# A two-layer decoder trunk on one NeuronCore: fewer side steps per unit of matmul, one attention block and half of a weight split moved to other stages

## Chip, cores and metric

The kernel runs on 1 core of one Trainium2 chip. The metric is the device time of one execution in microseconds (us); of several runs the median counts. One further execution was recorded by the hardware profiler, and all rows of the trace come from that one.

## What is computed

The reference is a residual stream of 2048 tokens of width 1024 that goes through two layers. Layer A is a gated MLP whose gate mixes the tokens of each chunk of 128 by a causal matrix. Layer B is attention in three groups of 8 heads with dilations 1, 4 and 16, each over a band of 128 keys back, with one shared set of keys and values; the three results are joined by a softmax over their log-sums. All of it is float32.

```python
# layer A
h = rms_norm(x, norm_g) * (1 + scale) + shift
u, v, z = split(h @ w_in, 3)                       # 1024 -> 3 x 2048
v = rms_norm(gelu(v), sgu_g)                       # then mixed over each chunk of 128 tokens
x = x + gate * ((gelu(u) * mixed(v) * silu(z)) @ w_out)
# layer B
k, v = split(h_kv @ w_kv, 2)                       # 6 heads each, rms_norm on k
q, z = split(h_b @ w_in)                           # 24 heads and 1024 for z, rms_norm on q
for g, d in enumerate((1, 4, 16)):                 # band attention on tokens taken d apart
    o[g], lse[g] = dilated_group_attn(q[g], k[g], v[g], d)
x = x + gate_b * ((sum(softmax(lse)[g] * o[g]) * silu(z)) @ b_w_out)
```

`shift`, `scale` and the gates come from a small product of `c`.

## The kernel before

**Quarters and products.** The 2048 tokens are taken in four quarters of 512; the code counts them from 0, this text from 1. For each quarter the kernel runs layer A, its output product (to x of layer B), then the shared keys and values, the queries of the three groups and z (`proj_B`, four blocks of 128 tokens each). Quarters 2 and 3 share their layer A (`layer_half`). Every float32 product is made of three matmuls: each operand is split (`split`, lines 272 and 273) by ScalarE into a rounded high part and by VectorE into the remaining low part, and high x high, low x high and high x low are added in PSUM (`mm3`, line 301). Most products are cut into 2 x 2 blocks and done with seven block products instead of eight, with weights `t1` to `t4` that are sums and differences of the blocks, written to memory beforehand.

**The stages that the change touches, in order of time:**
- `layer_half`: `dense_v` multiplies the v columns in two blocks (`b` = 4 and 5), seven products of 96 matmuls each. Then come eight gate groups `g`, each one `gate_block` for u and one for z, of seven products of 12 matmuls; their mixing matmuls (tile `pmh`, line 1468) read v once the norm over all v columns (`rvh`) is known.
- `layer_out(2)`: the output product of quarter 3 (`dense_o`, tiles `pd_o2a`, `pd_o2b`), seven products of 48 matmuls.
- `proj_B(2)`: keys and values (`kv_block`), and the queries of dilation 16 (`q_block(2)`), before `ahead` starts the loading of quarter 4's x into the only slot of the pool `one`.
- `layer_A(3)`: quarter 4's v products (`dense_s2`), then u and z (`dense_f`, lines 343 to 345, 16 blocks of 48 matmuls), then its output product.

**Side work.** What is not on the path of the current product is written as Python generators in the list `fillers`. Each `yield` ends a step. A product calls `tick(part)` after every few matmuls; it adds `rate[0] * part` to a counter and runs as many steps as the counter holds whole units, so that `rate[0]` is the number of steps per unit of tick. A unit is 24 matmuls in `dense_v`, `dense` and `dense_f` (0.25 per 6 matmuls), 12 matmuls in `gate_block` (0.25 per 3), and 21 in `dense_o`, `dense_s` and `dense_s2` (0.2857 per 6). `drain()` runs all steps that are left; `complete(g)` those of one generator. The steps set the order in which instructions are handed to a scheduler, which lays out each engine's queue and can let an instruction ahead whose data and buffer are there.

**The generators that matter here:**
- `combine_out` makes the weights `t1` to `t4` of layer A's output matrix: 8 items, each with two loads of 512 KB (tile `co`, line 451, issued one item ahead), four subtractions on VectorE (line 476), four splits (tile `cs`), and four stores of 512 KB (line 473). It has 2 steps before the first item and 3 per item. It is added behind the fifth product of block 4, once `sums_h` is complete, and is completed at gate group 2, where its pool gives way to the attention's (`ap`) and the generator `in_long` begins.
- `presplit` loads tiles of a weight matrix, splits them and stores both parts; `presplit_b` does that for layer B's output matrix (16 tiles `rawb` and `wbs`, to `wod`), which the last stage of the kernel reads.
- `attend` runs attention over blocks of 128 queries, two units (key heads) per block, in four stages per unit: `att_1` transposes keys and queries (tiles `kT`, `qT`), `att_2` makes scores and the exponentials (`ps`, `pr`), `att_3` transposes those (`pT`, finished by VectorE at line 1812 and GpSimd at 1813), `att_4` multiplies by the values (`po`, line 1838). Each stage is one step; the stages of different units interleave, so that three steps lie between `att_3` and `att_4` of a unit. Per call there are 4 x (units + 4) steps with the skew that is used here.
- `attend_local(Q, ..., both)` runs the four dilation-4 blocks of a quarter and, if `both`, the dilation-1 blocks behind them (`near`), for which `joint` first passes statistics through memory. With `both` false it runs only three of the four blocks.
- `earlier` runs beside quarter 4's u, z and output products: the fourth dilation-4 block of quarter 2 (`(1, 7)`), `joint(1)`, `near(1)`, then quarter 3's dilation 4 and 1. Every sixth step it also runs one of `presplit_b`. It holds 24 + 1 + 48 + 97 = 170 steps. The first three blocks of quarter 2's dilation-4 attention run in quarter 3's output product, 40 steps at rate 2.6.

Of the kernel before, what the change touches and what calls it, by code (L numbers as in the profile page):

```python
# [13 lines left out]
F32 = mybir.dt.float32  # L14
F32R = mybir.dt.float32r
# [20 lines left out]
def trunk(ctx, tc, out, x, c, a_ada_w, a_ada_b, a_norm_g, a_w_in, a_sgu_g, a_w_spatial,  # L36
# [387 lines left out]
                split(us[i - 1][:, 0, :], us[i - 1][:, 1, :], raws.pop(i - 1))  # L424
            yield

    def presplit_b():

        todo = [(b_w_out[k * P:(k + 1) * P, n * 512:(n + 1) * 512], wod[n, k]) for n in range(2) for k in range(KT)]
        return presplit(todo, own_tiles("b"))  # L430

    def own_tiles(nm):
        return lambda i, u: (wp.tile([P, 2, 512], F32R, tag="w", name=f"w{nm}s{i}") if u else
                             rp.tile([P, 512], F32, tag="raw", name=f"raw{nm}{i}"))
# [828 lines left out]
    def layer_A(Q, hA, m, sqv, j0):  # L1263
        if Q:
            ops, sums = sums_A(Q, hA, m)
            ev = [v_evac(Q, m, sqv, j) for j in range(4)]
            dense_s2(ops, (4, 5), f"v{Q}", lambda b, t, src, n: ev[2 * (b - 4) + n](t, src[:, 0:512]), sums)
            rate[0] = 4.9
        for j in range(j0, 0 if Q else 4):
            with ExitStack() as behind:  # L1270
                if Q == 0 and j == 1:
# [146 lines left out]
    def layer_half(ops, got):  # L1418

        nonlocal xp, ap_  # L1420
        ops.update({n: op_tile(n) for n in ("s2", "s1", "s4", "s3")})
        ops["22"] = op_tile("22", one)
        sqh.extend(sp.tile([P, 16], F32, tag="sqv", name=f"sqh{i}").rearrange("p (t j) -> p t j", t=4) for i in range(2))
        rvh = sp.tile([P, 16], F32, tag="sqv", name="rvh")[:, 0:8]
        sa = sums_h(ops, 12)
        next(sa)
        fillers.append(sa)
        co = combine_out()

        def others():  # L1430
            complete(sa)
            fillers.append(co)
            rate[0] = 1.3

        for b in (4, 5):
            rate[0] = 1.3
            dense_v(b, ops, lambda t, n, src, dst, junk, b=b: v_put(t, 2 * (b - 4) + n, src, dst, junk),
                    {} if b == 5 else {"22": others})
        store_late(0)
        for i in range(2):  # L1440
            nc.vector.tensor_reduce(rvh[:, 4 * i:4 * i + 4], sqh[i], AX.X, ALU.add)
        nc.gpsimd.tensor_scalar(rvh, rvh, 1.0 / AW, EPS, ALU.mult, ALU.add)
        nc.gpsimd.tensor_tensor(rvh, rvh, mhalf[:, 0:8], ALU.pow)
        rate[0] = 1.0
        for g in range(8):
            if g == 2:
                complete(co)
                cb.release()
                xp = None
                ap_ = ctx.enter_context(tc.tile_pool(name="ap", bufs=2, reuse_waits="tile"))  # L1450
                fillers.append(in_long())
                rate[0] = 1.5
            vch = []
            for half in range(2):
                v = wp.tile([P, 4, 256], F32, tag="w", name=f"vc{g}{half}")
                nc.sync.dma_start(v, vh[half * QT:(half + 1) * QT, g * 256:(g + 1) * 256]
                                  .rearrange("(c p) e -> p c e", p=P))
                for c in range(4):
                    i = 4 * half + c
                    nc.gpsimd.tensor_scalar(v[:, c, :], v[:, c, :], rvh[:, i:i + 1], None, ALU.mult)  # L1460
                vch.append(v)
            mt = {}

            def put_u(i, half, src):
                e = 2 * g + i
                pm = pst(f"pmh_{e}{half}")
                for c in range(4):
                    nc.tensor.matmul(pm[:, c * P:(c + 1) * P], vch[half][:, c, i * P:(i + 1) * P],
                                     wst[:, g, :], start=True, stop=True)
                m = mt[i, half] = sum_tile(f"mth_{e}{half}")[:, 0:512]  # L1470
                nc.vector.scalar_tensor_tensor(
                    m.rearrange("p (c t) -> p c t", t=P), pm.rearrange("p (c t) -> p c t", t=P),
                    late["sgu"][:, e:e + 1], late["b_s"][:, g, :].unsqueeze(1).broadcast_to([P, TPQ, P]),
                    ALU.mult, ALU.add)
                nc.scalar.activation(src, src, AF.Gelu_apprx_tanh)
                nc.vector.tensor_tensor(m, src, m, ALU.mult)

            def put_z(i, half, src):
                m = mt[i, half]
                nc.scalar.activation(src, src, AF.Silu)  # L1480
                if g == 7 and half == 0:
                    nc.vector.tensor_tensor(got["mt"][1][:, 6 + i, :], src, m, ALU.mult)
                    return
                nc.vector.tensor_tensor(m, src, m, ALU.mult)
                stores.append([0, lambda e=2 * g + i: nc.sync.dma_start(yd[half][:, e, :], m)])

            gate_block(g, 0, ops, put_u)
            gate_block(g, 1, ops, put_z, begin_y(got) if g == 7 else {})
        store_late(0)
# [65 lines left out]
    def proj_B(Q, hk, hb, keep, rest, ahead, ready):  # L1555
# [82 lines left out]
        if Q == 1:  # L1638
            rate[0] = 1.2
            slots = one.tile([P, 4, 2, 512], F32, tag="big", name="gbw")  # L1640
            fillers.append(delayed(ada_gate(b_ada_w[0], b_ada_b, 1, "gb", slots)))
        q_block(2)
        if Q == NQ - 1:
            fillers.append(wide_attention())
# [207 lines left out]

    def attend_local(Q, wrap=False, alt=False, both=True):

        bs = range(4 * Q, 4 * Q + (4 if both else 3))
        yield from attend([(1, b) for b in bs], wrap, int(alt), 1 + (wrap or alt), wrap or alt)
        if both:
            yield from joint(Q)
            yield from near(Q, wrap, alt)
# [198 lines left out]
    fillers.append(side_work())  # L2058
    rate[0] = 2.2
    def earlier():  # L2060
        p = presplit_b()
        for n, _ in enumerate(chain(attend([(1, 7)], True, 0, 2, True), joint(1), near(1, True), attend_local(2, True))):
            if n % 6 == 5:
                next(p, None)
            yield
        yield from p

    got, ops_h = {}, {}
    for Q in range(NQ):
        if Q in (0, 3):  # L2070
            if Q:
                one.release()
                xp = ctx.enter_context(tc.tile_pool(name="xp", bufs=4, side="right", reuse_waits="tile"))
                fillers.append(earlier())
                rate[0] = 0.0
            hk, hb, keep, rest, ahead_kv = layer_A(Q, hA, m, sqv, 1 if Q == 0 else 0)
        else:
            if Q == 1:
                layer_half(ops_h, got)
                drain()  # L2080
                rate[0] = 0.0
            else:
                fillers.append(attend_local(1, True, False, False))
                rate[0] = 2.6
            hk, hb, keep, rest, ahead_kv = layer_out(Q, got.pop("mt"), got.pop("yo", {}), got.pop("begun", None))
        if Q > 0:
            drain()
# [52 lines left out]
```

## Time and profile before

| | us |
|---|---|
| median of 3 runs (lowest to highest) | 2940.27 (2939.66 to 2943.56) |
| the profiled execution | 2939.51 |
| its span, first to last instruction | 2937.8 |
| TensorE busy in that span | 2863.8 (97%) |
| VectorE, ScalarE, GpSimd busy | 2216.8, 1639.8, 815.2 |

The mean granted clock of TensorE in that execution was 0.995. In the rows, PE is TensorE's matmuls, PEld its weight loads, DVE VectorE, ACT ScalarE, POOL GpSimd, SP the engine that issues all DMAs; `out<-in` are the program's tile names, and `L301` is line 301 of the kernel. A row of the groups ends with busy time, the mean ns of one instruction, and the engine's idle time just before the group, with who ended it. A row of the waits reads: engine, tile and line that waited, who released it, the sum of the waits in us, their count, the longest. Matmuls overlap in the pipeline: one of 512 columns is recorded with about 389 ns, while 24 of them in a row take about 5.4 us.

### The profile page before, as it was taken

The numbers are of one execution on the slowest core, as the hardware profiler recorded it, in microseconds if no ns is written. First come the engines' busy times: TensorE is split into PE (matmuls) and PEld (weight loads), VectorE is DVE, ScalarE is ACT, GpSimd is POOL, SyncE is SP. The second block draws the span as 40 slices with busy tenths as digits, with TensorE's granted clock in tenths as the row PEclk, the third lists the DMA queues.
The fourth block names the chain that finished last, engine by engine and source line by source line (L and its number), as shares of the span: only waits on it lengthen the run. The fifth ranks groups of instructions, "written<-read, shape, count | busy, mean of one in ns | idle before, by whom it ended". The sixth has DMA issues, their size and how long they took to land.

```text
span 2937.8 us, 45193 instructions
## 1 busy us (share of the span) xinstructions
PE 2863.8 (97%) x14450; PEld 2392.8 (81%) x14450; DVE 2216.8 (75%) x4104; ACT 1639.8 (56%) x3335; POOL 815.2 (28%) x1085
## 2 busy tenths in 40 slices
PE   8999999999999999999999999999999999999999
PEld 5888888877778887877888888878888888888887
DVE  6878567787677789867786868878879676888682
ACT  4334355766546666544553657756757367876441
POOL 1066513330021125003324035024435111122212
PEclk9999999999999999999999999999999999999999
DMA  9899856888945655687989768854636967789653
GB/s 322 293 332 343 293 188 206 277 294 298 325 164 163 208 175 170 234 326 224 311 302 320 237 201 268 286 181 155 213 105 230 353 203 231 251 271 331 222 169 111
DMA packets 388210, 718.74 MB, mean 245 GB/s; under 512 B 42011, under 2 KB 121085, under 8 KB 387589
## 3 DMA queue, kind: packets, MB, share of 16 engines
q1 hardware_dynamic: 387972, 715.87, 72.5%
q8 instruction: 114, 1.87, 0.3%
q14 instruction: 124, 1.01, 0.1%
HBM read 541.52 MB, written 174.20 MB: 244 GB/s over the span
## 4 chain that ended last, share of the span: by engine, by line
PE 73%; DVE 9%; DMA 7%; issue 4%; ACT 3%; POOL 2%; SPq 1%; POOLq 0%; DVEq 0%; ACTq 0%
PE pd_kv L301 7%; PE po L1838 3%; PE pd_o L301 3%; PE pd_v L301 2%; PE pd_z L345 2%; PE pd_z L344 2%; PE pd_z L343 2%; PE pd_o3a L301 1%; PE pd_u L345 1%; PE pd_u L343 1%; PE pd_u L344 1%; PE pd_v3a L301 1%; PE pd_vh4a L301 1%; PE pd_o1a L301 1%; PE pd_v3b L301 1%
## 5 line engine op out<-in xcount | busy, mean ns | idle before, releaser
L301 PE MATMUL pd_kv<-w_kv,hkh 128*128 128x512 f32 x672 | 209.5, 392 | 2.2 <-DVE w_kv L273 2.1
L1838 PEld LDWEIGHTS po<-kv,pT 128*128 128x128 f32 x1200 | 149.9, 193 | 30.6 <-POOL pT L1813 17.9
L1838 PE MATMUL po<-kv,pT 128*128 128x128 f32 x1200 | 156.2, 279 | 18.6 <-POOL pT L1813 14.2
L301 PEld LDWEIGHTS pd_kv<-w_kv,hkh 128*128 128x128 f32 x672 | 125.0, 188 | 29.6 <-DVE w_kv L273 3.2
L301 PE MATMUL pd_kv<-w_kv,hkl 128*128 128x512 f32 x336 | 131.0, 390 | 0.0
L1778 ACT ACTIVATE pr<-pr,stat,rt 128x256 f32<-128x256 f32 (+1 forms) x192 | 104.3, 545 | 40.0 <-DVE stat L1772 27.1
L1604 POOL TENSOR_SCALAR s_q<-s_q 128x4 f32<-128x4 f32 x96 | 25.8, 269 | 342.9 <-DVE s_q L1603 279.7
L272 ACT ACTIVATE w_q<-raw_q 128x512 fp32r<-128x512 f32 x144 | 88.5, 627 | 51.5 <-PE pd_kv L301 10.5
L273 DVE TENSOR_TENSOR w_q<-raw_q,w_q 128x512 fp32r<-128x512 f32 x144 | 97.4, 698 | 23.4 <-ACT w_q L272 22.8
L1460 POOL TENSOR_SCALAR vc<-vc,rvh 128x256 f32<-128x256 f32 x64 | 61.3, 975 | 190.1 <-DMA vc<-vh 138.2
L2029 PE MATMUL pf<-wo,yb 128*128 128x512 f32 x256 | 104.5, 408 | 0.2 <-ACT yb L1992 0.2
L343 PE MATMUL pd_u<-hAh,w_u 128*128 128x512 f32 x256 | 103.6, 405 | 0.0
L343 PE MATMUL pd_z<-hAh,w_z 128*128 128x512 f32 x256 | 103.6, 405 | 0.0
L2031 PE MATMUL pf<-wo,yb 128*128 128x512 f32 x256 | 100.8, 394 | 0.0
L345 PE MATMUL pd_z<-hAh,w_z 128*128 128x512 f32 x256 | 100.6, 393 | 0.0
L344 PE MATMUL pd_z<-hAl,w_z 128*128 128x512 f32 x256 | 100.5, 392 | 0.0
L344 PE MATMUL pd_u<-hAl,w_u 128*128 128x512 f32 x256 | 100.4, 392 | 0.0
L345 PE MATMUL pd_u<-hAh,w_u 128*128 128x512 f32 x256 | 100.4, 392 | 0.0
L2030 PE MATMUL pf<-wo,yb 128*128 128x512 f32 x256 | 100.1, 391 | 0.0
L1778 ACT ACTIVATE st_pr<-st_pr,stat,rt 128x256 f32<-128x256 f32 (+1 forms) x128 | 73.5, 576 | 38.0 <-DVE stat L1772 19.3
L1786 POOL TENSOR_TENSOR dg<-pr,ident 128x256 f32<-128x256 f32 x38 | 29.2, 768 | 212.2 <-ACT pr L1778 165.3
L1813 POOL TENSOR_TENSOR pT<-pT,dg 128x256 f32<-128x256 f32 x76 | 64.5, 852 | 78.3 <-DVE pT L1812 75.1
(1474 smaller groups left out, 9005.2 us busy)
## 6 DMA issues: line engine op xcount, KB each, us to landing
raw_q<-in_b_w_in_dram SPq DMA_DIRECT2D x144, 256.0 KB, 3.8
qt<-qd SPq DMA_DIRECT2D x96, 260.0 KB, 4.2
od<-ot SPq DMA_DIRECT2D x96, 256.0 KB, 3.1
w_o<-wtd SPq DMA_DIRECT2D x48, 512.0 KB, 5.4
raw_kv<-in_w_kv_dram SPq DMA_DIRECT2D x84, 256.0 KB, 3.6
kv<-kvd SPq DMA_DIRECT2D x75, 256.0 KB, 5.1
raw_u<-in_a_w_in_dram SPq DMA_DIRECT2D x64, 256.0 KB, 4.1
wt<-st_cw SPq DMA_DIRECT2D x64, 256.0 KB, 5.5
```

Of the source, the lines that this page charges most:

```text
L272: nc.scalar.activation(hi, src, AF.Copy)
L273: nc.vector.tensor_tensor(lo, src, hi.bitcast(F32), ALU.subtract)
L301: last_mm[0] = nc.tensor.matmul(pt, a, u[:, w, :], start=f, stop=e, skip_group_check=more)
L343: nc.tensor.matmul(pts[i], wh, hh[:, k, :], start=k == 0, stop=False)
L344: nc.tensor.matmul(pts[i], wh, hl[:, k, :], start=False, stop=False)
L345: nc.tensor.matmul(pts[i], wl, hh[:, k, :], start=False, stop=k == KT - 1)
L1778: nc.scalar.activation(pr[:, i, :], pr[:, i, :], AF.Exp, bias=mneg[:, i:i + 1], scale=u["rt"][:, h:h + 1], accum_out=lsum[:, i:i + 1])
L1813: nc.gpsimd.tensor_tensor(pT[:, :, 0, :], pT[:, :, 0, :], u["dg"][:, c * hp:(c + 1) * hp, :], ALU.add)
L1838: nc.tensor.matmul(po[:, h * P:(h + 1) * P], u["pT"][h // hp][:, h % hp, j, :], u["kv"][:, j, kh, 1, :], start=j == 0, stop=j == nk - 1)
L2029: nc.tensor.matmul(pt, yb[:, 0, k, :], w_[:, 0, :], start=k == 0, stop=False)
L2030: nc.tensor.matmul(pt, yb[:, 0, k, :], w_[:, 1, :], start=False, stop=False)
L2031: nc.tensor.matmul(pt, yb[:, 1, k, :], w_[:, 0, :], start=False, stop=k == KT - 1)
```

## The change

Five edits:
1. In `layer_half`, the rate is 1.3 for block 4, 0.8 from the point where `combine_out` is added to the end of block 5 (1.3 before), and 0.55 in gate groups 0 and 1 (1.0 before).
2. `attend_local` runs all four blocks also with `both` false, so block 7 of dilation 4 goes from quarter 4's u product (`earlier`) to quarter 3's output product, whose rate goes from 2.6 to 3.1.
3. `presplit_b` takes one column half `n`. Half 0 runs in quarter 3's `proj_B` beside `q_block(2)` and `kv_block(0)` at rate 0.8 (1.7 before, with nothing left to run), in a tile of the pool `one` (`spare_tiles`) instead of the weights' own buffers. Half 1 stays in `earlier`.
4. `earlier` holds 1 + 48 + 97 = 146 steps and runs one of `presplit_b` every tenth.
5. The rate in quarter 4's u and z products goes from 4.9 to 4.0.

```diff
-    def presplit_b():
-
-        todo = [(b_w_out[k * P:(k + 1) * P, n * 512:(n + 1) * 512], wod[n, k]) for n in range(2) for k in range(KT)]
-        return presplit(todo, own_tiles("b"))
+    def presplit_b(n, tiles):
+
+        return presplit([(b_w_out[k * P:(k + 1) * P, n * 512:(n + 1) * 512], wod[n, k]) for k in range(KT)], tiles)
+
+    def spare_tiles():
+        t = one.tile([P, 8, 512], F32R, tag="big", name="pre")
+        return lambda i, u: (t[:, 4 + 2 * (i % 2):6 + 2 * (i % 2), :] if u else t[:, i % 4, :].bitcast(F32))
...
             dense_s2(ops, (4, 5), f"v{Q}", lambda b, t, src, n: ev[2 * (b - 4) + n](t, src[:, 0:512]), sums)
-            rate[0] = 4.9
+            rate[0] = 4.0
...
         def others():
             complete(sa)
             fillers.append(co)
-            rate[0] = 1.3
-
+            rate[0] = 0.8
+
+        rate[0] = 1.3
         for b in (4, 5):
-            rate[0] = 1.3
             dense_v(b, ops, lambda t, n, src, dst, junk, b=b: v_put(t, 2 * (b - 4) + n, src, dst, junk),
...
-        rate[0] = 1.0
+        rate[0] = 0.55
         for g in range(8):
...
+        if Q == 2:
+            rate[0] = 0.8
+            fillers.append(presplit_b(0, spare_tiles()))
         q_block(2)
...
-        bs = range(4 * Q, 4 * Q + (4 if both else 3))
+        bs = range(4 * Q, 4 * Q + 4)
         yield from attend([(1, b) for b in bs], wrap, int(alt), 1 + (wrap or alt), wrap or alt)
...
     def earlier():
-        p = presplit_b()
-        for n, _ in enumerate(chain(attend([(1, 7)], True, 0, 2, True), joint(1), near(1, True), attend_local(2, True))):
-            if n % 6 == 5:
+        p = presplit_b(1, own_tiles("b"))
+        for n, _ in enumerate(chain(joint(1), near(1, True), attend_local(2, True))):
+            if n % 10 == 9:
                 next(p, None)
...
                 fillers.append(attend_local(1, True, False, False))
-                rate[0] = 2.6
+                rate[0] = 3.1
```

## The prediction

> **What bounds the kernel now.** I read the page's totals and chain first, then stage windows, then matmul groups and waits inside the stages that the change touches.
>
> ```profile
> span 2937.8 us, 45193 instructions
> PE 2863.8 (97%) x14450; PEld 2392.8 (81%) x14450; DVE 2216.8 (75%) x4104; ACT 1639.8 (56%) x3335; POOL 815.2 (28%) x1085
> PE 73%; DVE 9%; DMA 7%; issue 4%; ACT 3%; POOL 2%; SPq 1%; POOLq 0%; DVEq 0%; ACTq 0%
> ```
>
> TensorE is busy for 2863.8 of 2937.8 us. The change neither adds nor removes a matmul, so what it can win is inside the 74 us in which TensorE stands idle, plus what a lowered clock costs after such idle time. The profiled execution took 2939.51 us, 1.7 more than its span and 0.8 under the median 2940.27. The windows say where those 74 us lie (columns: window, length, then busy us of PE, PEld, DVE, ACT, POOL, granted clock, DMA share, GB/s):
>
> ```profile
> 680.00:720.00 40.00, 38.13 (x161) 30.77 (x160) 27.89 (x45) 23.09 (x49) 0.00 (x0) 0.96 0.80 280
> 720.00:780.00 60.00, 59.24 (x261) 48.73 (x260) 43.09 (x69) 35.34 (x71) 0.00 (x0) 1.00 0.92 328
> 780.00:820.00 40.00, 30.53 (x115) 24.31 (x114) 21.84 (x37) 20.46 (x42) 9.95 (x10) 0.83 0.80 287
> 804.00:871.00 67.00, 62.24 (x289) 51.99 (x288) 47.96 (x77) 28.87 (x49) 18.63 (x18) 0.95 0.51 179
> 820.00:890.00 70.00, 70.00 (x341) 59.02 (x340) 51.72 (x82) 27.77 (x44) 16.26 (x16) 1.00 0.45 153
> 960.00:1215.00 255.00, 247.66 (x1327) 209.72 (x1326) 217.30 (x432) 155.33 (x286) 66.73 (x80) 0.99 0.57 190
> 1520.00:1640.00 120.00, 116.72 (x621) 98.32 (x620) 84.75 (x161) 52.50 (x115) 36.93 (x56) 0.99 0.88 313
> 1677.00:1740.00 63.00, 63.00 (x279) 52.17 (x279) 40.97 (x66) 34.79 (x62) 21.75 (x44) 1.00 0.61 190
> 1930.00:2245.00 315.00, 299.40 (x1775) 259.58 (x1774) 261.28 (x601) 200.98 (x403) 135.13 (x190) 0.99 0.52 166
> 1940.00:1950.00 10.00, 7.65 (x38) 6.56 (x38) 8.91 (x17) 2.87 (x4) 0.21 (x1) 0.83 0.46 143
> 2245.00:2340.00 95.00, 93.89 (x477) 79.14 (x478) 70.75 (x144) 42.26 (x84) 25.19 (x30) 1.00 0.91 337
> ```
>
> Output combinations run from 680 to 820: 12.1 us of idle TensorE (1.9 + 0.8 + 9.5), and a clock of 0.96 and 0.83. Quarter 4's u and z products with attention beside them, 1930 to 2245, hold 15.6 us. Quarter 3's output product (1520 to 1640) holds 3.3, and the dilation-16 query product with the first keys (1677 to 1740) none. (The code counts quarters from 0; I say quarter 1 to 4.)
>
> **Part 1, combinations at fewer steps.** Matmul groups between 680 and 820 (busy us, mean ns | idle before), then two waits of the same stretch:
>
> ```profile
> L301 PE MATMUL pd_vh5a<-w_vh5t,op 128*128 128x512 f32 x24 | 8.2, 505 | 4.7 <-ACT w_vh5t L272 4.7
> L301 PE MATMUL pd_vh4a<-w_vh4t,ops 128*128 128x512 f32 x24 | 7.6, 479 | 1.9 <-ACT pd_vh4a L1405 1.9
> L301 PE MATMUL pd_vh5a<-w_vh,ops 128*128 128x512 f32 x24 | 5.9, 396 | 0.8 <-DVE w_vh L273 0.8
> L301 PE MATMUL pd_vh4a<-w_vh4t,op 128*128 128x512 f32 x24 | 5.6, 389 | 0.0
> L1468 PE MATMUL pmh<-wst,vc 128*128 128x128 f32 x4 | 1.4, 459 | 4.8 <-POOL vc L1460 4.8
> ```
> ```profile
> DVE co L476 <- DMA co<-in_a_w_out_dram: 11.5, 8, 3.5
> ACT w_vh5t L272 <- DVE co L476: 5.8, 1, 5.8
> ```
>
> An undisturbed run of 24 matmuls takes 5.6 us. The first two rows take 8.2 and 7.6, so 2.6 and 2.0 us of lowered clock ride on their 4.7 and 1.9 us of idle time. The cause is in the waits: VectorE waits 11.5 us for combination loads, and what is queued behind it (weight splits, evacuations) comes late. Removable here: 4.7 + 2.6, and 1.9 + 2.0 + 0.8, 12.0 in all. The 4.8 before pmh stays: it waits for the norm of the last v column, which the change does not touch.
>
> How far the new rates thin the stream:
>
> ```profile
> 720.15 5.44 PE pd_vh5a L301 x24
> ```
>
> Here 24 matmuls, which are one unit of tick in the v products, last 5.44 us; a gate block's unit is 12 matmuls, 2.72. A combination item is 3 steps: 3 / 1.3 x 5.44 = 12.6 us before, 3 / 0.8 x 5.44 = 20.4 after, in the gate blocks 3 / 0.55 x 2.72 = 14.8. Loads are issued one item ahead, so they get 7.8 us more to land. I take the 7.3 us around pd_vh5a as gone, and half of the other 4.7, since the first items run ahead of their place in the program and would meet the same traffic: -9.6.
>
> Against that, work moves. Of 26 steps, 4 x 1.3 + 14 x 1.3 = 23.4 were over by the end of the v products; now 4 x 0.8 + 14 x 0.8 = 14.4 are. The rest takes 11.6 / 0.55 = 21 of the 28 units of the first two gate groups: (26 - 14.4) / 3 = 3.9 items, in about 67 us from 804 to 871. Per item there are four subtractions and four splits' subtractions:
>
> ```profile
> L273 DVE TENSOR_TENSOR cs<-co,cs x32: 678/682/694, 706.4 to 819.2; 128x512 fp32r<-128x512 f32 x32
> L476 DVE TENSOR_TENSOR co<-co x16: 680/691/693, 683.4 to 791.1; 128x512 f32<-128x512 f32 x16
> ```
>
> Thus 4 x 0.69 + 4 x 0.68 = 5.5 us of VectorE, 21.4 for 3.9 items. The window 804 to 871 has 47.96 already, 2.7 of it from combinations, so about 66.7 of 67 would be filled. Part can slide into 720 to 780 (43.09 of 60) or past 871. The lower bound of the loss is 0, as in 820 to 890 (51.72 of 70, no idle); the upper comes from 960 to 1215, where VectorE is 85% busy and TensorE loses 7.3 us: at 85%, 66.7 needs 78.5 us, a loss of 11.5. I take 5. Part 1: -4.6.
>
> **Part 2, the dilation-4 pair leaves quarter 4.** Block 7 is two units. It now stands alone at the head of quarter 4's attention:
>
> ```profile
> 1943.48 0.80 PE L1764 MATMUL ps<-kT,qT 128*128 128x256 f32 x2 [2.35 <-DVE kT L1721]
> 1962.77 1.16 PE L1838 MATMUL po<-kv,pT 128*128 128x128 f32 x8 [1.46 <-POOL pT L1813]
> 1965.41 1.16 PE L1838 MATMUL po<-kv,pT 128*128 128x128 f32 x8 [1.48 <-POOL pT L1813]
> 1608.83 2.08 PE L1838 MATMUL po<-kv,pT 128*128 128x128 f32 x8 [1.74 <-POOL pT L1813]
> ```
> ```profile
> L1838 PE MATMUL po<-kv,pT 128*128 128x128 f32 x344 | 44.9, 281 | 12.0 <-POOL pT L1813 11.9
> L1838 PE MATMUL po<-kv,pT 128*128 128x128 f32 x96 | 13.6, 290 | 2.0 <-POOL pT L1813 2.0
> ```
>
> Its three waits, 5.3 us, leave quarter 4 with it. So does the low clock after the first, 0.83 over 1940 to 1950: 1.7 us, of which I count 1.5. The other waits of po there are 11.9 - 2.9 = 9.0 us over 344 / 16 = 21.5 less 2 units, 0.46 each, with three steps of 5.44 / 4.9 between pT and po, 3.33 us. In quarter 3's output product (a unit of tick is 21 matmuls, 4.76 us) three steps are 3 x 4.76 / 2.6 = 5.49 us, and 96 / 16 = 6 units lose 2.0, 0.33 each. At rate 4.0 the three steps are 4.08 us. By geometry each of eight waits would shrink by 0.75, 6.0 in all; by the line through the two rows it is 0.05 over 19.5 units, 0.9. I take 1.5, near the rows: spacing plainly isn't all of it. Quarter 4: -8.3 (ends -6.8 and -12.8).
>
> In quarter 3's product the three steps shrink to 3 x 4.76 / 3.1 = 4.61 us for 8 units: by the same line 0.39 x 8 = 3.1, 1.1 more than 2.0, and the enlarged tail (as at 1608.83) makes it +2. Ends: 0, and 8 x 1.12 (9.0 over eight waits) - 2.0 + 1.7 of clock, +8.7.
>
> **A rule against the rows.** The row at 1943.48 has 2.35 us of idle, and the clock falls all the same. The Trainium skill, "TensorE: Matmul & The Clock Gate", sections "What's actually happening" and "HAM oscillation — how this bites in real kernels", says that the clock halves after an idle window of about 3.4 us and asks only that no gap exceed that. By that rule neither the pair nor the 1.9 us before pd_vh4a would cost clock, and the sum would be 2.5 us smaller: 2932. The trace disagrees, so the sum keeps the rows.
>
> **Part 3, half of the last weights in layer B.** Eight of sixteen splits move from quarter 4 to 1677 to 1740:
>
> ```profile
> L273 DVE TENSOR_TENSOR wbs<-rawb,wbs 128x512 fp32r<-128x512 f32 x16 | 11.6, 726 | 2.7 <-ACT wbs L272 2.7
> L1042 SPq DMA_DIRECT2D xa<-in_x_dram x4: 327/428/430, 1641.8 to 1643.1; - x4
> L1049 ACT ACTIVATE sqj<-xa x8: 616/622/624, 1738.3 to 1767.0; 128x512 f32<-128x512 f32 x8
> L858 PE MATMUL pt_a<-ident,xa x32: 270/272/273, 1802.4 to 1842.9; 128*128 128x128 f32 x32
> ```
>
> Eight times 0.73 brings VectorE there to 46.8 of 63, 74%, the share at which 820 to 890 lost nothing: 0. ScalarE has 34.79 of 63 and room for as many. The new tile takes the one slot that quarter 4's x now enters at 1642, so those four loads go behind the last store, near 1740, and on SP the next query weights queue behind them. ScalarE's squares start some 10 us later; TensorE needs their result at 1802, 35 us after the last square, so the cover holds. Were it gone, the delay of 10 us would be paid. The u and z products have 32 units of tick, so quarter 4's own output product is left with 146 - 32 x 4.0 = 18 steps instead of 170 - 32 x 4.9 = 13; it idles for 1.1 us in 95 now. I give both together +0.5; ends 0 and +4.
>
> **Sum.** -4.6 - 8.3 + 2 + 0.5 = -10.4 on 2939.51, 2929.1; with 0.8 for the median, **2930**. Less than 0.2%, 5.9 us, can't be told from no change.
>
> **Rivals.** (a) Nothing is paid back: the gate blocks and quarter 3 absorb the moved work free and all 12.0 go. -12.0 - 12.8, 2916. For it: 820 to 890 has no idle time at all. Against: 66.7 of 67 us on VectorE.
> (b) The rates do not do what they say: a rate fixes only the place in the program's order, and loads and subtractions are let ahead as slots come free (the first subtraction runs at 683.4, and block 5 only begins at 720.15). The combination waits stay, 5 is paid in the gate blocks only where work really moved (say 2), and the result is -8.3 + 2 + 0.5 + 2, 2936.5, within what can't be told from no change.
> (c) Slower: VectorE becomes the bound of the first two gate groups. Price 11.5, and the clock at 0.83 as in 780 to 820 over those 78 us, 13 more, in place of 5: -10.4 + 19.5 = +9.1, 2949. It decides once the gate groups lose over 5 + 10.4 + 5.9 = 21 us. For it, the full 67 us; against it, 85% cost only 7.3 us in 255, with 0.99 of the clock.
>
> **Chances.** Forecast 0.52 (its own range 2922 to 2938), (a) 0.17, (b) 0.17, (c) 0.11, others 0.03. Faster by over 0.2%, below 2934.4: some 0.42 of the first, (a), and 0.05 of (b), 0.64; within: 0.22; slower: (c) and the tails of the others, 0.14. Range 2917 to 2944: it takes in nearly all of (a), and of (c) the half where the price stays under 20.
>
> **What would show it.** Right: no wait of ACT for co, idle before pd_vh5a under 1 us, clock near 1 from 780 to 800; combinations until about 870 with some idle TensorE in the gate groups; no kT wait near 1943; po idle in 1930 to 2245 near 8 us; no idle at 1677 to 1740. Wrong: combination waits at the same places, over 10 us idle between 815 and 890, or po waits in quarter 3's product of over 5 us.

## The result, and the profile after

The changed kernel takes 2908.44 us (median of 4 runs, 2903.27 to 2911.30), the kernel before 2941.91 beside it on the same chip (4 runs, 2939.66 to 2946.48): a ratio of 0.9882 with a 95% interval of 0.9862 to 0.9902. The forecast was 2930.0 and its range began at 2917: the direction was right, but the gain is over three times the one forecast, and even rival (a), where nothing is paid back, stopped at 2916. The profiled execution took 2910.12 us, with a mean granted clock of 0.998 (0.995 before).

The page's totals and chain of the kernel after:

```profile
span 2908.3 us, 45236 instructions
PE 2851.9 (98%) x14450; PEld 2386.6 (82%) x14450; DVE 2205.5 (76%) x4104; ACT 1639.2 (56%) x3335; POOL 819.7 (28%) x1085
PE 79%; DVE 6%; DMA 5%; ACT 4%; issue 4%; POOL 1%; SPq 0%; POOLq 0%; ACTq 0%; DVEq 0%
```

The span is 29.5 us shorter. TensorE's idle time (span less PE) fell from 74.0 to 56.4, by 17.6; its busy time fell by 11.9 with the same 14450 matmuls. Most of the latter is clock, by an estimate from the two mean clocks: 0.3% of 2908 is 8.7 us. VectorE's share of the chain fell from 9% to 6%.

The windows that answer to the prediction's, kernel after (columns as there):

```profile
680.00:720.00 40.00, 37.22 (x156) 30.05 (x155) 23.80 (x38) 19.97 (x43) 0.00 (x0) 0.96 0.68 227
720.00:780.00 60.00, 60.00 (x266) 49.70 (x265) 39.02 (x61) 35.21 (x71) 0.00 (x0) 1.00 0.83 295
780.00:820.00 40.00, 37.59 (x171) 30.75 (x170) 30.32 (x49) 22.52 (x48) 12.39 (x10) 1.00 0.92 311
798.00:865.00 67.00, 64.59 (x309) 53.87 (x308) 64.00 (x103) 36.93 (x64) 22.36 (x18) 1.00 0.78 276
1507.00:1628.00 121.00, 116.86 (x654) 100.31 (x653) 88.36 (x175) 56.56 (x128) 47.90 (x68) 0.97 0.89 309
1675.00:1735.00 60.00, 60.00 (x266) 49.71 (x265) 42.94 (x71) 34.69 (x64) 19.51 (x40) 1.00 0.90 306
1931.00:2209.00 278.00, 277.35 (x1647) 241.27 (x1646) 229.72 (x540) 177.50 (x358) 117.59 (x166) 1.00 0.48 155
```

The 9.5 us of idle time and the 0.83 of the clock at 780 to 820 are gone, and so is nearly all idle time of quarter 4's u and z products: 0.65 us in 278, against 15.6 in 315. Idle time is left at 680 to 720 (2.8 us, 1.9 before), before pmh (within 798 to 865) and in quarter 3's output product, which has a lower clock than before (0.97, it was 0.99).

A fixed window holds other work after the change, so the sum is made by stages, each from its first product to the first product of the next. Kernel before: block 5 of the v products, gate groups 1 and 2, gate groups 7 and 8, quarter 3's output product, quarter 4's u, z and output products.

```profile
719.99:804.71 84.72, 79.25 (x338) 64.63 (x336) 58.17 (x93) 48.10 (x98) 0.00 (x0) 0.96 0.93 328
804.71:895.33 90.62, 85.86 (x402) 71.83 (x400) 63.61 (x102) 37.89 (x63) 26.22 (x26) 0.96 0.46 159
1102.54:1214.27 111.73, 106.31 (x566) 89.47 (x564) 100.42 (x202) 63.92 (x116) 36.97 (x45) 0.98 0.55 187
1519.83:1677.29 157.46, 153.67 (x790) 128.95 (x789) 114.39 (x212) 76.18 (x161) 38.72 (x60) 0.99 0.85 295
1931.42:2384.89 453.47, 435.81 (x2446) 373.57 (x2445) 366.13 (x801) 269.18 (x537) 164.33 (x228) 0.99 0.61 204
```

The same five of the kernel after:

```profile
722.29:798.45 76.16, 76.16 (x338) 63.08 (x336) 46.75 (x74) 44.33 (x90) 0.00 (x0) 1.00 0.86 297
798.45:885.50 87.05, 84.64 (x401) 70.60 (x400) 77.13 (x125) 44.20 (x75) 29.69 (x26) 1.00 0.69 242
1093.95:1202.33 108.38, 105.40 (x565) 89.40 (x564) 98.44 (x203) 67.08 (x118) 42.23 (x48) 0.98 0.58 200
1507.41:1675.45 168.04, 163.41 (x865) 138.63 (x864) 126.40 (x241) 83.06 (x180) 51.91 (x76) 0.98 0.82 279
1931.07:2355.20 424.13, 420.83 (x2370) 361.49 (x2368) 342.61 (x763) 250.83 (x505) 154.75 (x212) 1.00 0.59 199
```

| stage | before | after | change | forecast |
|---|---|---|---|---|
| v products, blocks 4 and 5 | 165.16 | 157.27 | -7.9 | -9.6 |
| gate groups 1 and 2 | 90.62 | 87.05 | -3.6 | +5 |
| gate groups 7 and 8 | 111.73 | 108.38 | -3.4 | 0 |
| quarter 3's output product, and quarter 4's u, z and output | 610.93 | 592.17 | -18.8 | -6.3 |
| all else | | | +4.2 | +0.5 |

The last two stages are added up, because the pair that moved takes its own matmuls along: 75 of them now run in one and no longer in the other. "All else" is small differences over many stages. Single recordings differ by as much where the code is the same: block 4 of the v products takes 78.15 to 82.27 us in the ten that run it as the kernel after does, and all that follows quarter 4's output product takes 542.87 and 553.29 us in two of one kernel.

### The profile page after: what moved, and what is told of

It reads as the page before. It is cut to its first block, busy times and chain, and to the rows that moved or that the text cites. A ratio compares the mean times of both kernels' runs of the same rounds, so it can differ in the third digit from the quotient of the medians.

```text
span 2908.3 us, 45236 instructions
## 1 busy us (share of the span) xinstructions
PE 2851.9 (98%) x14450; PEld 2386.6 (82%) x14450; DVE 2205.5 (76%) x4104; ACT 1639.2 (56%) x3335; POOL 819.7 (28%) x1085
## 4 chain that ended last, share of the span: by engine, by line
PE 79%; DVE 6%; DMA 5%; ACT 4%; issue 4%; POOL 1%; SPq 0%; POOLq 0%; ACTq 0%; DVEq 0%
PE pd_kv L301 8%; PE po L1844 4%; PE pd_o L301 3%; PE pd_v L301 2%; PE pd_z L345 2%; PE pd_z L344 2%; PE pd_z L343 2%; PE pd_u L343 2%; PE pd_u L345 2%; PE pd_u L344 2%; PE pd_o3a L301 1%; PE pd_v3b L301 1%; DMA qt<-qd 1%; PE pf L2035 1%; PE pf L2037 1%
```

## The experiments

Theories at the start: **the prediction's** (combination loads that land late; a line through two stages for the spacing), against **a queue** (in block 5 the weight loads stand behind the combination's DMAs on SP) and **a distance** (a wait before po appears only where the chain of work from `att_3` to pT outlasts the time that three steps give it, so one rate decides over nearly all of the waits). In the expectations theory S is this distance, theory L the load of the eight splits that left quarter 4, and theory P the pair that stood alone.

### One part undone, from the kernel after

The rate of quarter 4's u and z products back at 4.9:

```diff
-            rate[0] = 4.0
+            rate[0] = 4.9
```

> The changed kernel with one number set back: 4.9 steps per unit of tick in quarter 4's u and z products instead of 4.0. Theory S (spacing): attention's last product waits when the chain behind the transposes (5.3 us on average before, 4.7 after) is longer than its distance in the queue (5.2 before, 6.0 after), so the closer steps alone bring most of the waits back: 6 to 12 us of idle TensorE in u and z, 2917 to 2922. Theory L (load): the eight weight splits that left made the chain short, so with them gone the rate hardly matters: under 3 us of idle, 2908 to 2912. Theory P (the lone pair): under 3 us as well.

Ratio to the kernel before 0.9916 (0.9892 to 0.9940). Its quarter 4 stages:

```profile
1926.20:2362.18 435.98, 425.37 (x2370) 363.85 (x2368) 344.41 (x763) 248.01 (x502) 148.63 (x212) 0.99 0.58 194
```

435.98 against 424.13: the same instructions take 11.9 us longer, 7.3 of it idle TensorE (10.61 against 3.30). Four waits before po hold 6.2 us of the idle time, one of them 4.1. This is what theory S expected, and the one number is worth more than the whole gain forecast, 10.4, of which it was given 1.5. The stages are read from one recorded execution each; in whole runs the difference is 0.0034, 10 us, with intervals that overlap.

All sixteen splits back in quarter 4, one every sixth step (`presplit_all` does what `presplit_b` did in the kernel before):

```diff
-            fillers.append(presplit_b(0, spare_tiles()))
...
-        p = presplit_b(1, own_tiles("b"))
+        p = presplit_all()
...
-            if n % 10 == 9:
+            if n % 6 == 5:
```

> The changed kernel with all sixteen splits of the last weights back in quarter 4 (one every sixth step, in the weights' own buffers) and none in layer B. Theory L: the po waits come back, 6 to 12 us of idle TensorE in u and z, 2917 to 2922. Theory S: at most 3 us, 2908 to 2913. Either way the stretch of the dilation-16 queries stays without idle time.

Ratio 0.9889 (0.9874 to 0.9903), where the kernel after has 0.9862 to 0.9902. Quarter 4's stages take 426.81 (+2.7), the two stages together 592.21 (592.17 after). That is theory S again. With the pair gone and the rate at 4.0, the place of the splits is worth 2 to 3 us in quarter 4 (the six recordings that run quarter 4 as the kernel after does take 423.71 to 424.81) and nothing that shows in whole runs.

The pair back in quarter 4, at the head of `earlier` (the output product's rate goes up so that the steps still end with the product):

```diff
-        bs = range(4 * Q, 4 * Q + 4)
+        bs = range(4 * Q, 4 * Q + (4 if both else 3))
...
-        for n, _ in enumerate(chain(joint(1), near(1, True), attend_local(2, True))):
+        for n, _ in enumerate(chain(attend([(1, 7)], True, 0, 2, True), joint(1), near(1, True), attend_local(2, True))):
...
-                rate[0] = 3.1
+                rate[0] = 2.6
...
-            rate[0] = 2.0
+            rate[0] = 2.7
```

> The changed kernel with block 7's two units back at the head of quarter 4's attention; quarter 3's output product gets its old rate 2.6, and quarter 4's output product 2.7 instead of 2.0, so that the 170 steps end within it. Theory P: the three waits and the low clock return, 5.3 + 1.5 us, and the others with them if the pair displaced what followed; quarter 3's product wins 2 to 3; in all 2912 to 2916. Theories S and L: about 2 to 4 us of the pair's own waits and none of the others, less what quarter 3's product wins: 2907 to 2911.

Ratio 0.9862 (0.9847 to 0.9877): undoing this part costs nothing, and perhaps it gains, which no theory expected. The last set comes back to it.

The combinations back at 1.3 and 1.0:

```diff
-            rate[0] = 0.8
+            rate[0] = 1.3
...
-        rate[0] = 0.55
+        rate[0] = 1.0
```

> The changed kernel with the combinations back at 1.3 steps per unit through block 5 and 1.0 in the gate groups. If the thinner stream alone freed block 5, its 8.5 us come back there and some 3 before the first mixing matmul: 2919 to 2922, with the stages behind gate group 2 unchanged. If part of it is the queue's order having changed for other reasons, less than 5 us: 2908 to 2913.

Ratio 0.9930 (0.9915 to 0.9945): 0.0048 above the kernel after, 14 us. Block 5, then gate groups 1 and 2, then 7 and 8 take 82.52, 93.77 and 113.62 us, against 76.16, 87.05 and 108.38: 18.3 in all. The third of these stages begins some 280 us behind the last combination, and no theory named it. Part of the second is spread: the six recordings with the thick stream's code there take 90.4 to 93.8 us.

### One part done, from the kernel before

The rate alone (4.0, and 2.7 in the output product behind it, so that the steps end there):

```diff
-            rate[0] = 4.9
+            rate[0] = 4.0
...
-            rate[0] = 2.0
+            rate[0] = 2.7
```

> The kernel before with one thing changed: 4.0 steps per unit in quarter 4's u and z products (and 2.7 instead of 2.0 in its output product, so that all 170 steps end there). Theory S: the po waits of the later units go, 6 to 9 us won, 2931 to 2936. Theory L: under 2 us won, 2938 to 2942, since all sixteen splits are still there.

Ratio 0.9954 (0.9941 to 0.9966), 13.5 us. Quarter 4's stages:

```profile
1932.36:2374.41 442.05, 433.38 (x2445) 371.43 (x2444) 364.96 (x801) 260.31 (x532) 163.49 (x228) 1.00 0.64 210
```

-11.4, of it 9.0 of idle time (17.66 to 8.67). The po waits of its u and z products, then those of the kernel before and of the kernel after, show what went:

```profile
L1838 PE MATMUL po<-kv,pT 128*128 128x128 f32 x288 | 35.6, 275 | 0.4 <-POOL pT L1813 0.4
```
```profile
L1838 PE MATMUL po<-kv,pT 128*128 128x128 f32 x352 | 46.1, 281 | 12.2 <-POOL pT L1813 12.2
```
```profile
L1844 PE MATMUL po<-kv,pT 128*128 128x128 f32 x288 | 35.0, 275 | 0.0
```

12.2 us of waits become 0.4 by the rate alone, with the pair still in place. (At 4.0 some units that ran here run in the output product instead, so there are 18 of them and not 22. That product's idle time goes from 2.0 to 6.0 us, only 0.8 of it before po.) The gain is more than theory S expected, 6 to 9 us.

The pair alone (block 7 out of `earlier` and into quarter 3's output product, at rate 3.1), and the splits alone (half of them in layer B, the rest every tenth step), each with the change's own lines for it:

```diff
-        bs = range(4 * Q, 4 * Q + (4 if both else 3))
+        bs = range(4 * Q, 4 * Q + 4)
...
-        for n, _ in enumerate(chain(attend([(1, 7)], True, 0, 2, True), joint(1), near(1, True), attend_local(2, True))):
+        for n, _ in enumerate(chain(joint(1), near(1, True), attend_local(2, True))):
...
-                rate[0] = 2.6
+                rate[0] = 3.1
```

> The kernel before with block 7's pair alone moved to quarter 3's output product at rate 3.1. Theory P: 5.3 + 1.5 us and more leave quarter 4, 2 to 3 come to quarter 3: 2930 to 2937. Theories S and L: the pair's place is taken by the next units, which wait as much: 2938 to 2942.

```diff
+            fillers.append(presplit_b(0, spare_tiles()))
...
-            if n % 6 == 5:
+            if n % 10 == 9:
```

> The kernel before with eight of the sixteen weight splits moved to layer B beside the dilation-16 queries. Theory L: quarter 4's waits fall by 6 or more, 2930 to 2935. Theory S: by less than 2, 2938 to 2942. Nothing is lost at the dilation-16 queries in either.

The pair: 0.9980 (0.9967 to 0.9993), 5.9 us; quarter 4's stages get 12.5 us shorter, quarter 3's product 6.3 longer. This is what theory P expected; S and L had nothing won. The splits: 1.0001 (0.9989 to 1.0013), and 453.39 against 453.47 in quarter 4, against theory L.

The combinations alone:

```diff
-            rate[0] = 1.3
+            rate[0] = 0.8
...
-        rate[0] = 1.0
+        rate[0] = 0.55
```

> The kernel before with the thinner combination stream alone. The prediction's own sum for this part was 4.6 us won (9.6 won in the v products, 5 lost in the gate groups). If the gate groups take the work for nothing, as the trace of the changed kernel suggests, 11 to 13 us: 2928 to 2931. If what was seen there hangs on the other edits, 2935 to 2938.

Ratio 0.9931 (0.9905 to 0.9957), 20.3 us. The three stages:

```profile
723.08:799.24 76.16, 76.16 (x337) 63.06 (x336) 46.82 (x75) 44.48 (x90) 0.00 (x0) 1.00 0.87 297
799.24:886.13 86.89, 84.56 (x402) 70.59 (x400) 77.12 (x125) 44.30 (x75) 29.62 (x26) 1.00 0.69 242
1093.91:1199.99 106.08, 103.62 (x566) 88.10 (x564) 98.28 (x203) 66.85 (x118) 41.93 (x48) 1.00 0.60 202
```

-8.6, -3.7 and -5.6, 17.9 in all, in line with the 18.3 that undoing it cost. It is more than the 11 to 13 us expected. The rest lies in stages of unchanged code: quarter 3's output product takes 153.31 us instead of 157.46, block 4 takes 82.27 instead of 80.44.

### What is behind these numbers: one execution each, from the kernel after

Each of these four kernels was executed once (2919.18, 2918.44, 2914.65 and 2905.01 us in this order, with 2940.80 for the kernel before), so only their stages are read.

Why gate groups 7 and 8? All steps after the combinations run by one counter, and what is left in it decides which small group of matmuls each later step follows. The thick stream leaves 0.798 in it, the thin one 0.198. This kernel keeps the thick stream and changes only that remainder, where `in_long` begins:

```diff
-            rate[0] = 0.8
+            rate[0] = 1.3
...
-        rate[0] = 0.55
+        rate[0] = 1.0
...
                 rate[0] = 1.5
+                rate[1] = 0.19812
```

> The changed kernel with the thick combination stream (1.3 and 1.0), and the step counter's fraction set to 0.198 where attention joins the gate groups, as the thin stream leaves it (the thick one leaves 0.798). In the runs so far gate groups 6 and 7 took 111.7 to 113.6 us with the thick stream and 106 to 108.4 with the thin one, though no combination is left there. If the fraction alone shifts attention's steps against the gate products and so makes the difference: 106 to 108.5 for the two groups, block 5 still at 82 to 85. If it comes from the combinations' later end (buffers, stores): 111 to 114.

Gate groups 7 and 8:

```profile
1103.06:1210.72 107.66, 104.95 (x565) 89.45 (x564) 98.39 (x203) 67.25 (x118) 40.91 (x47) 0.98 0.59 201
```

107.66, where the thick stream had 113.62; the kernels with the thin stream's remainder have 106.0 to 108.4, all others 111.7 to 113.6. Block 5 stays at 83.15. So some 3 to 6 us of the gain have nothing to do with combinations and came by luck: they are the place at which later steps happen to fall. Which of those steps matters was not taken apart.

Does VectorE bind the gate groups (rival (c))? Here more combinations are pushed into them, 0.4 steps in block 5 and 0.73 in the groups; and, in the second kernel, fewer, 0.8 and then 1.0 steps, so that the stream ends early but comes thick:

```diff
-            rate[0] = 0.8
+            rate[0] = 0.4
...
-        rate[0] = 0.55
+        rate[0] = 0.73
```

> The changed kernel with 0.4 steps per unit through block 5 and 0.73 in the gate groups, so that 18.8 of 26 steps, some 6.3 items and 34 us of VectorE, fall into the first two groups, beside about 56 us that it has there anyway, in 81 us of matmuls. If a full VectorE binds there as the slow rival said: the two groups take 90 to 100 us instead of 87.1, with waits for weight splits. If weights are split far enough ahead for that not to matter, or the queue lets the work go ahead of its place: 86 to 89.

```diff
-        rate[0] = 0.55
+        rate[0] = 1.0
```

> The changed kernel with 1.0 steps per unit in the gate groups (as before) but 0.8 in block 5. If the 0.8 alone frees block 5: 76.2 us there, and 1.0 in the gate groups costs at most 2. If the lower rate behind it matters too, because its items are let ahead into block 5: 78 to 84 us.

Gate groups 1 and 2, of the first and of the second:

```profile
799.88:889.77 89.89, 85.95 (x401) 71.50 (x400) 83.81 (x137) 48.00 (x82) 30.87 (x23) 0.98 0.84 299
```
```profile
795.29:887.68 92.39, 87.09 (x401) 71.27 (x400) 77.92 (x125) 43.57 (x75) 30.71 (x26) 0.98 0.65 227
```

The first takes 2.8 us more than the 87.05 of the kernel after, just between my two expectations, with VectorE 93% busy over 90 us. But the only wait of TensorE there is the one before pmh, in the first 24 us (3.9 us, 2.3 in the kernel after). Where VectorE is fullest, TensorE has no idle time:

```profile
824.00:854.00 30.00, 30.00 (x142) 25.10 (x142) 29.50 (x48) 16.67 (x28) 10.34 (x8) 1.00 0.89 321
854.00:889.77 35.77, 35.77 (x175) 30.19 (x174) 34.61 (x57) 19.39 (x32) 5.05 (x5) 1.00 0.84 295
```

The thick stream, with the same VectorE work as the kernel after (77.92 and 77.13), takes 5.3 us more: TensorE waits 2.2 us before pmh and 3.1 for ScalarE's splits of gate weights. So it is not the amount of VectorE work that costs. That those splits come late because the combinations come more closely fits, but was not taken apart. My expectation for the second, at most 2, missed. Block 5 takes 76.16 in both.

The distance theory says that waits shrink along a curve: strongly at first, then not at all once the distance covers the chain. A rate halfway tells that from a straight line:

```diff
-            rate[0] = 4.0
+            rate[0] = 4.45
```

> The changed kernel with 4.45 steps per unit in quarter 4's u and z, halfway between before and after. Quarter 4 from u through its output product took 424.1 us at 4.0 and 436.0 at 4.9. By a wait that is the excess of the chain over the distance, with the chain's length spread from 2.6 to 7.8 us, the loss rises faster than the rate: 426 to 429, po waits of 1 to 3 us. By a straight line: 430 to 431.

```profile
1924.83:2353.61 428.78, 422.02 (x2369) 362.03 (x2368) 345.72 (x763) 250.81 (x505) 153.22 (x212) 1.00 0.59 197
```

424.13, 428.78 and 435.98 at 4.0, 4.45 and 4.9: the first half of the way costs 4.7 us, the second 7.2. A straight line would put the halfway kernel at 430.1. It lies 1.3 us under that, hardly more than the 1.1 us by which the six recordings at 4.0 differ: it leans to a curve and does not prove one.

### Is there a better version? The pair again, on one chip

The kernel after, and the kernel with the pair back (edit as above), timed side by side:

> The changed kernel once more, beside the next one on the same chip: 2903 to 2912.

> The changed kernel with the pair back in quarter 4 (rates 2.6 and 2.7 in the two output products). If moving the pair was worth what the prediction gave it at the new rate (its own three waits and the low clock, 6.8, less 2 in quarter 3): some 5 us slower than the changed kernel. If it only exchanges one place for another: within 3 us of it. If the fuller output product of quarter 3 costs more than the pair's waits did at 4.0 steps: 4 to 8 us faster.

0.9867 (0.9851 to 0.9884) and 0.9878 (0.9856 to 0.9900), medians of 2903.42 and 2907.84: no difference clear of the intervals. Quarter 3's output product and quarter 4's stages, first of the kernel after:

```profile
1503.75:1670.40 166.65, 161.81 (x865) 137.13 (x864) 126.94 (x241) 83.02 (x179) 51.97 (x76) 0.99 0.82 280
1926.57:2350.79 424.22, 420.99 (x2369) 361.64 (x2368) 342.07 (x763) 251.32 (x505) 156.04 (x212) 1.00 0.59 200
```
```profile
1506.65:1660.42 153.77, 151.37 (x789) 127.63 (x788) 115.64 (x211) 75.02 (x159) 39.73 (x60) 1.00 0.85 293
1915.59:2352.55 436.96, 431.45 (x2446) 370.66 (x2444) 358.10 (x793) 256.74 (x525) 163.13 (x228) 1.00 0.60 197
```

The sums are 590.87 and 590.73. At the rate of 4.0, moving the pair carries 12.9 us of work and waits from one stage into the other and wins nothing. The better ratio of the first run of this version did not repeat, and none of these kernels is clearly faster than the changed one.

## Why the prediction was wrong, point by point

**The failed step is the spacing in quarter 4**, "By geometry each of eight waits would shrink by 0.75, 6.0 in all; by the line through the two rows it is 0.05 over 19.5 units, 0.9. I take 1.5, near the rows: spacing plainly isn't all of it." Measured: 11.4 from the kernel before, 11.9 from the kernel after, beyond even the upper end, 6.0. The line went through two stages that differ in more than spacing, and it took the mean wait per unit to fall evenly with distance. The 3.33 us between pT and po counted the product's matmuls alone; attention's own run in between as well.

From the timelines of u and z I took, for each attention unit, the time from the end of its transposes to the end of GpSimd's second pT (the chain) and to the start of its po matmuls (the distance), and their means: before 5.3 and 5.2 us, with the rate at 4.0 alone 5.1 and 5.8, after 4.7 and 6.0, with the rate back 5.4 and 5.3, at 4.45 5.3 and 5.6. Single chains last 2.7 to 10.4. At 4.9 chain and distance are about equal on the mean, and in the kernel before 11 waits before po fall in 22 units; 0.6 us more distance puts most of them in the clear. Idle time is only part of it: the same matmuls are busy 2.4 us less in the first pair of kernels (435.81 and 433.38) and 4.5 less in the second (425.37 and 420.83), at a clock of 1.00 instead of 0.99. In the kernel after the chain is shorter as well, but with all sixteen splits back it is as long as before, 5.3 us, at a distance of 6.1, and the waits before po are only 1.6 us: the distance is enough.

One thing no run separates. At 4.0 a tick of six matmuls runs exactly one step (0.25 x 4.0), and no distance is under 4.0 us; at 4.45 and 4.9 some ticks run two, and the shortest distances are 2.6. Whether the mean distance counts or the even placing stays open.

**The pair.** The rows were right: the wait for kT near 1943 and the two of po behind it are gone, and alone, at 4.9, the move wins 6.2 us over both stages (12.5 less 6.3; forecast 6.8 less 2). But the parts aren't a sum. Both stages together take 610.9 us before, 599.7 with the rate, 604.7 with the pair, 610.9 with the splits, 592.2 with rate and pair, 590.7 and 592.6 with rate and splits and no move of the pair, 603.0 with pair and splits, and 588.0 to 592.2 in the six recordings that have all three. Rate and pair add up, and the splits then bring 0 to 4 us more. The splits bring nothing alone but 7 to 9 us on top of the rate, and then the pair brings nothing. By these sums pair and splits take away much the same. The comparison isn't clean: the kernels made from the kernel after also hold the thin combination stream, which alone takes the two stages to 607.8.

**Quarter 3's output product**, forecast +2 of waits: its idle time goes from 3.8 to 4.6 us, and 9.7 of its 10.6 us more are busy time, the pair's own matmuls and a clock of 0.98 instead of 0.99. The stage isn't steady: with the pair's move alone it takes 163.77 us, and with the thin combinations alone, its own code untouched, 153.31 instead of 157.46. Why was not taken apart.

**Block 5: right in size, wrong in cause.** Forecast -7.3 at pd_vh5a, measured -8.6; with another cause, the size is luck. The reasoning was that combination loads get longer to land, so that VectorE no longer waits for them. It still waits just as long, in the waits of 672 to 860 of the kernel after (11.5 before):

```profile
DVE co L479 <- DMA co<-in_a_w_out_dram: 12.3, 7, 3.1
```

And ScalarE's 5.8 us for a combination's subtraction, which the prediction took for the cause of the gap at 791, end 40 us ahead of it:

```profile
751.07 1.93 ACT L272 ACTIVATE w_vh5t<-raw_vh5t 128x512 fp32r<-128x512 f32 x3 [5.79 <-DVE co L476]
```

What changed is SP's order. The timeline before, SP's issues, then the splits of ScalarE and VectorE with TensorE's first use between them (start, length, then engine, line and tile):

```profile
778.71 3.13 SPq L473 DMA_DIRECT2D wtd<-cs  x4
781.89 2.45 SPq L451 DMA_DIRECT2D co<-in_a_w_out_dram  x2
784.39 2.08 SPq L280 DMA_DIRECT2D raw_vh5t<-wt  x4
...
790.55 2.46 ACT L272 ACTIVATE w_vh5t<-raw_vh5t 128x512 fp32r<-128x512 f32 x4 [1.28 <-DMA raw_vh5t<-wt]
791.24 1.22 PE L301 MATMUL pd_vh5a<-w_vh5t,op 128*128 128x512 f32 x2 [4.71 <-ACT w_vh5t L272]
791.68 2.49 DVE L273 TENSOR_TENSOR w_vh5t<-raw_vh5t,w_vh5t 128x512 fp32r<-128x512 f32 x4
```

and the same after, with TensorE's first use behind them:

```profile
756.92 0.92 SPq L280 DMA_DIRECT2D raw_vh5t<-wt  x2
763.31 4.84 SPq L476 DMA_DIRECT2D wtd<-cs  x4
768.20 0.42 SPq L454 DMA_DIRECT2D co<-in_a_w_out_dram  x1
768.72 1.26 SPq L280 DMA_DIRECT2D raw_vh5t<-wt  x2
...
781.18 0.69 DVE L273 TENSOR_TENSOR w_vh5t<-raw_vh5t,w_vh5t 128x512 fp32r<-128x512 f32 x1 [0.35 <-ACT w_vh5t L272]
...
787.57 0.61 PE L301 MATMUL pd_vh5a<-w_vh5t,op 128*128 128x512 f32 x2
```

Before, the four weight loads of the last product are issued behind four stores and two loads of the combinations, at 784.39. ScalarE's part of their splits waits for them to land and starts at 790.55, and TensorE has its 4.7 us of idle time before pd_vh5a waiting for ScalarE. VectorE's part, behind the combinations, comes only after that. In the kernel after, the loads go out 16 to 27 us earlier, two of them ahead of an item's stores, and the splits end 5.7 us before TensorE uses the first. All ten recordings (of eight kernels) with 0.8 or fewer steps in block 5 have 76.16 us and no idle time there. That the scheduler puts the loads ahead because fewer combination steps precede them is inferred from the order. Block 4, counted on for half of the other 4.7, won nothing: 80.44 and 81.11, and its gap near 697 stays. (A product of the v columns holds 48 matmuls, as block 5's row shows with 338 for seven products, not the 96 stated at the start; the prediction's units go by 48.)

**Gate groups 1 and 2, forecast +5, measured -3.6.** The work did move: the last combination's subtraction is at 854 instead of 819, and VectorE is busy for 64.00 of 67 us, nearly the 66.7 that I worked out. But full is not late. The only idle time of TensorE there is the wait before pmh, 2.4 us instead of the 4.8 that the prediction had as staying. Rival (c) needed a price for a full VectorE, taken from a stage of 85% that loses time for reasons of its own; with VectorE 97 and 98% busy from 824 to 890, in the rows above, no price shows. Rival (b) falls as well, since the combinations did spread.

**Gate groups 7 and 8** weren't in the sum at all; their 3.4 us came with the counter's remainder. **The splits** at 1675 to 1735 cost nothing, as forecast: no idle time there, and the cover of x held.

**The clock.** I said that the trace contradicts the rule of the Trainium skill, "TensorE: Matmul & The Clock Gate", section "What's actually happening", by which the clock halves after some 3.4 us of idle time. The kernel after contradicts it again, in quarter 3's output product, its timeline and then its windows:

```profile
1517.46 1.95 PE L301 MATMUL pd_o2a<-w_o,yo 128*128 128x512 f32 x6 [1.82 <-DMA w_o<-wtd]
```
```profile
1518.65:1522.05 3.40, 3.40 (x11) 2.73 (x10) 0.00 (x0) 0.00 (x0) 0.00 (x0) 0.50 1.03 417
1522.05:1526.00 3.95, 3.95 (x24) 3.36 (x24) 2.02 (x5) 2.68 (x4) 0.00 (x0) 1.00 1.05 397
```

After 1.82 us of idle time the granted clock is 0.50 for 3.4 us and then full again: this gap costs its length and, by an estimate from these rows, 1.7 us more. Not every such gap does. In the granted clock of the sixteen recorded executions, the low spells of each start on one grid of 3.41 us. From 640 us on, of the grid steps at full clock, 52 of the 53 in which TensorE was idle for over 1.9 us are followed by a low one, 18 of the 50 with 1.5 to 1.9 us, and 1 of some 10,000 with less. What counts is the idle time within one step of the grid, and a gap that falls across two steps can go free.

## What to carry to other kernels

Where side work runs so many steps ahead of its use, compare the chain from producer to use with the time those steps span, unit by unit: when the two are about equal, a small change of the rate is worth many waits, and edits that shorten the chain or lengthen the distance act on the same ones, so their gains don't simply add up. Before a wait is put down to a slow load, look at what stood ahead of that load in the queue that issues it. And where one counter places all side steps, an edit early on shifts every later one: a stage that moves without being touched can be tested by setting the counter's remainder alone.

## What the runs showed of the hardware that was not expected

VectorE can be 96 to 98% busy for 30 us and more (64.00 of 67, 29.50 of 30, 34.61 of 35.77) while TensorE, fed from its splits, has no idle time but an older wait before pmh; the same VectorE work in thicker bursts went with 5.3 us more.

A queue that issues DMAs in order also passes its waits on. In the kernel after, a store of the combinations takes 0.33 us to issue at the median; the 4.84 us of the four above are mostly waits for VectorE's splits, and two weight loads stand behind them. Issuing itself can be slow, too: the two combination loads before took 2.45 us, at a DMA share of 1.03 in that stretch, where the median of one is 0.44. And the clock follows the idle time within steps of a fixed grid of 3.41 us, as told above.
